# Seven block products for eight in the second MLP product of a diffusion block

## The chip, the cores and the metric

The kernel runs on one core of one Trainium2 chip. The metric is the device time in microseconds from start to end, as a median over runs. The engines are TensorE (PE, its weight loads PEld), VectorE (DVE), ScalarE (ACT), GpSimd (POOL) and SyncE (SP), on whose queue all of this kernel's transfers are started.

## The reference, cut to what matters

One block works on 1024 tokens of width 1024 in float32: a mixer (state space and attention) and then a squared-ReLU MLP of width 4096. The change touches the MLP alone:

```python
def sq_relu_mlp(h, w1, b1, w2, b2):
    return jnp.square(jax.nn.relu(h @ w1 + b1)) @ w2 + b2

h2_l = modulate(rms_norm(x, norm2_g[l]), sh2_l, sc2_l)
x = x + g2_l * sq_relu_mlp(h2_l, w_mlp1[l], b_mlp1[l], w_mlp2[l], b_mlp2[l])
```

`g2_l` is one row of 1024 gates, the last part of the modulation, which the kernel computes from `c` and `w_mod`. Call s the squared ReLU, 1024 tokens by 4096.

## The kernel before

**Exact products from rounded ones.** A float32 operand is split in two: ACT copies it to the rounded type (H), and Pool, or DVE where `low=V`, subtracts H from the raw tile to give the rest (L). Each product then takes three matmuls, H by H, H by L and L by H (`mm3`, L143 to L145, and `prod`, L1641 to L1643). `wtile` (L135, L136) loads a tile and splits it, with a row of gates multiplied in first if `scale_row` is given (L134). `wsplit` (L1665, L1666) does it for the first MLP matrix and `mq_split` (L1737, L1738) for the second. Raw tiles `wr` have three buffers, `wH` and `wL` four each. Sums come into PSUM tiles from `mmc()`, which has six buffers.

**First MLP matrix.** The 4096 columns are 32 tiles of 128, taken in 16 pairs. For 14 pairs (`NA`) the 2 x 2 block product of a pair is made with seven products instead of eight. A first pass, `first(p)`, makes two of the seven, those with the blocks B11 and B21 of h2. A second pass, `mlp1(p)`, makes the other five: T2, T1, T3, B22, T4. A turn of it is this: DVE builds from two raw weight tiles the sums `cs` (two halves, L1691 and L1692), `c4` (L1694) and `wr` (L1695); ACT and Pool split them; TensorE runs five groups of 12 matmuls; DVE forms u2, u4 and u3 (L1699 to L1702) and three `r` (L1658), ACT applies ReLU and square, and SP stores `r` to DRAM (`s_d`). `cs` and `c4` have one buffer each, so that the sums of the next pair wait until Pool has split those of the last one. In names of the listings, c is `c4`.

**Second MLP matrix.** The 32 tiles of s come back from DRAM in 15 blocks `BL`: tile 0, tile 1, 13 pairs, and the last four together. A block takes 16 PSUM groups (8 token tiles by two halves of the columns), and DVE adds each to `acc2` (L1766). In the last block it then multiplies by `g2row` (L1768) and adds the residual x2 (L1769), and SP stores the output. Between blocks 3 and 7 `mod2` makes the last part of the modulation: eight loads of 512 KB into `wr` and a DVE multiply-add after each (L1256, L1258).

**Order.** The program is written as one stream; a scheduler sets the order on each engine, and each engine runs its list in order and waits at the head of it. In the first pass TensorE's order is the written one.

Of the kernel before, what the change touches and what calls it, by code (L numbers as in the profile page):

```python
# [48 lines left out]
def block_kernel(ctx, tc, io, out, dbg=None):  # L49
# [1668 lines left out]
    def w2_src(ft):  # L1718
        return w2[ft * 128:(ft + 1) * 128, :].rearrange("p (a n) -> p a n", a=1)

    def s_src(ft):
        return s_d[ft].rearrange("p (a n) -> p a n", a=1)

    pre = [(wtile(s_src(0), (1, 1024)), wtile(w2_src(0), (1, 1024)))]
# [16 lines left out]
    def mlp2_tiles(ft):
        rs = wload(s_src(ft), (1, 1024))
        rw_ = mq.tile([128, 1024], F32, name="rw2", tag="rw2", bufs=3)
        LD.dma_start(rw_.rearrange("p (a b) -> p a b", a=1), w2_src(ft))
        return mq_split(rs, "s", 6), mq_split(rw_, "w", 6)

    BL = [[0], [1]] + [[b, b + 1] for b in range(2, 28, 2)] + [[28, 29, 30, 31]]
    NBL = len(BL)
    pre2 = [(mq_split(wload(s_src(1), (1, 1024)), "f", 2), mq_split(wload(w2_src(1), (1, 1024)), "f", 2))]
    m2_todo = list(range(30, 40))  # L1750
# [55 lines left out]
```

## Time and profile before

| | us |
|---|---|
| median of three runs | 1913.58 (1910.86 to 1914.25) |
| the profiled execution | 1909.88 |
| its span, first to last instruction | 1908.2 |
| TensorE busy | 1841.1 (96%) |
| DVE, Pool and ACT busy | 1279.1 (67%), 895.4 (47%), 691.9 (36%) |
| second pass of the first MLP matrix | about 1330 to 1543 |
| second MLP matrix, with the end | 1543 to 1908 |

The profile is one execution, read with the start of its first instruction at 0. A row of the timeline gives the start, the duration, the engine, the line, the operation with output and inputs, and in brackets how long the engine stood before it and who ended that. The granted clock (PEclk) is a share of TensorE's full 2.4 GHz; it is 0.985 over the span.

### The profile page before, as it was taken

The page shows a single profiled execution, that of the slowest core. Times are in us where ns is not written, and L with a number is a line of the kernel's source. Part 1 is how long each engine was busy: PE and PEld are TensorE (multiplying, and loading weights), DVE is VectorE, ACT ScalarE, POOL GpSimd, SP SyncE. Part 2 cuts the span into 40 slices and gives each one's busy share as a digit, 9 for nine tenths or more (in the row PEclk, how much of TensorE's full clock was granted, in tenths as well). Part 3 has the DMA queues.
Part 4 walks back from the last instruction along what each step waited for, and adds up shares of the span by engine and source line. Part 5 has one row for each costly group of instructions (what it writes and reads, how often), then busy time and mean ns, then how long its engine had stood idle before and what let it go on. Part 6 is the DMA issues. An engine that isn't in the chain of part 4 may idle for free. (4 is left out here: it accounts for less than half of the span.)

```text
span 1908.2 us, 25109 instructions
## 1 busy us (share of the span) xinstructions
PE 1841.1 (96%) x9250; PEld 1402.6 (74%) x9250; DVE 1279.1 (67%) x2194; ACT 691.9 (36%) x1016; POOL 895.4 (47%) x471
## 2 busy tenths in 40 slices
PE   7889999998999999999989999999999999999998
PEld 4668888887776556556547777887888877878887
DVE  5989998738897787777645455486454457545556
ACT  4542222244314555555442121455444541111110
POOL 2232333313425777777784453375444564443330
PEclk9989999999999999999999999999999999999999
DMA  9412222221222000000006664355554465333213
GB/s 308 97 56 71 76 77 78 76 85 46 84 71 78 18 23 23 23 23 18 22 13 207 213 209 144 116 177 182 155 155 152 126 218 178 110 107 104 89 55 144
DMA packets 179339, 200.72 MB, mean 105 GB/s; under 512 B 28112, under 2 KB 128260, under 8 KB 179216
## 3 DMA queue, kind: packets, MB, share of 16 engines
q1 hardware_dynamic: 179216, 199.11, 32.6%
q8 instruction: 73, 1.20, 0.3%
q14 instruction: 50, 0.41, 0.1%
HBM read 154.85 MB, written 44.09 MB: 104 GB/s over the span
## 5 line engine op out<-in xcount | busy, mean ns | idle before, releaser
L1202 POOL TENSOR_TENSOR accP<-accP,P 128x1024 f32<-128x1024 f32 x96 | 240.9, 2510 | 20.9 <-ACT P L1184 15.7
L1766 DVE TENSOR_TENSOR acc<-acc,mm 128x512 f32<-128x512 f32 x240 | 162.5, 686 | 127.6 <-PE mm L145 127.6
L136 POOL TENSOR_TENSOR wL<-wr,wH 128x1024 fp32r<-128x1024 f32 (+1 forms) x58 | 135.9, 2351 | 197.9 <-ACT wH L135 187.0
L1184 ACT ACTIVATE P<-sT 128x1024 f32<-128x1024 f32 x160 | 163.8, 1026 | 116.6 <-PE sT L1180 114.1
L1088 DVE TENSOR_REDUCE m<-mx 128x1 f32<-128x512 f32 x240 | 154.5, 686 | 76.1 <-PE mx L1086 69.7
L143 PE MATMUL mm<-wH,sH 128*128 128x512 f32 x480 | 187.3, 390 | 1.3 <-DVE acc L1766 1.2
L144 PE MATMUL mm<-wL,sH 128*128 128x512 f32 x480 | 186.8, 389 | 0.0
L145 PE MATMUL mm<-wH,sL 128*128 128x512 f32 x480 | 186.7, 389 | 0.0
L1197 PE MATMUL pv<-P,Vt 128*64 128x512 f32 x640 | 150.5, 600 | 0.0
L1738 POOL TENSOR_TENSOR sL<-wr,sH 128x1024 fp32r<-128x1024 f32 x30 | 72.2, 2406 | 152.0 <-ACT sH L1737 152.0
L135 ACT ACTIVATE wH<-wr 128x1024 fp32r<-128x1024 f32 (+1 forms) x62 | 61.9, 1005 | 216.2 <-PE mm L144 96.4
L1737 ACT ACTIVATE sH<-wr 128x1024 fp32r<-128x1024 f32 x30 | 31.6, 1054 | 226.5 <-issue 160.7
L1177 PE MATMUL sT<-Q,KH 128*128 128x512 f32 x320 | 105.3, 410 | 2.2 <-ACT P L1184 2.2
L143 PEld LDWEIGHTS mm<-wH,sH 128*128 128x128 f32 x480 | 90.1, 188 | 22.5 <-DVE acc L1766 2.9
L145 PEld LDWEIGHTS mm<-wH,sL 128*128 128x128 f32 x480 | 90.1, 188 | 18.9
L144 PEld LDWEIGHTS mm<-wL,sH 128*128 128x128 f32 x480 | 90.1, 188 | 18.2
L143 PE MATMUL mm<-hH,wH 128*128 128x512 f32 x248 | 101.1, 408 | 0.0
L1180 PE MATMUL sT<-Q,K 65*128 65x512 f32 x320 | 100.9, 396 | 0.0
L145 PE MATMUL mm<-hH,wL 128*128 128x512 f32 x248 | 97.7, 394 | 0.0
L144 PE MATMUL mm<-hL,wH 128*128 128x512 f32 x248 | 97.3, 392 | 0.0
L1197 PEld LDWEIGHTS pv<-P,Vt 128*64 128x64 f32 x640 | 41.7, 136 | 71.6 <-issue 62.3
L1666 POOL TENSOR_TENSOR wL<-wr,wH 128x1024 fp32r<-128x1024 f32 x32 | 76.8, 2405 | 36.6 <-ACT wH L1665 36.6
...
## 6 DMA issues: line engine op xcount, KB each, us to landing
...
```

The costliest lines, as they stand in the source:

```text
L136: (low or G).tensor_tensor(L[:, :n], raw[:, :n], H[:, :n], op=OP.subtract)
L143: T.matmul(ps, lH, rH, start=i == 0, stop=False)
L144: T.matmul(ps, lH, rL, start=False, stop=False)
L145: T.matmul(ps, lL, rH, start=False, stop=i == n - 1)
L1088: V.tensor_reduce(m3[:, 4 * j + t, c:c + 1], m, axis=AX.X, op=OP.max)
L1177: T.matmul(o, KH[kv][:, ks], Q1[:, j], start=True, stop=False)
L1180: T.matmul(o, K2[kv][:, ks], Q2[:, j], start=False, stop=True)
L1184: S.activation(P, sT, AF.Exp, scale=HD ** -0.5)
L1197: T.matmul(pv[64 * j:64 * j + 64, :], Vt[:, kt, kv * 64:kv * 64 + 64], P[:, j * 512:(j + 1) * 512], start=kt == 0, stop=kt == NK - 1)
L1202: G.tensor_tensor(accP, accP, P, op=OP.add)
L1666: (low or G).tensor_tensor(L[:, :n], raw[:, :n], H[:, :n], op=OP.subtract)
L1766: V.tensor_tensor(a_, a_ if bi else bb2[:, o], ps, op=OP.add)
```

## The change

The second MLP product gets the same treatment. Tiles 0 to 27 of s and the rows of w2 that belong to them are cut into seven blocks of 512 rows (`NB`). Each block takes seven products of 24 matmuls (four PSUM groups of six), with operands A11, A12, A22 and S1 to S4 on the side of s and B11, B21, B22 and T1 to T4 on the side of w2. The last four tiles are multiplied plainly.

- *Sums of s.* `mlp1(p)` for p below 14 reads A11 back (stored by the first pass), and builds S3 on Pool and S1, S2, S4 on DVE (L1727), which are stored to DRAM; A21 isn't stored any more. ReLU and square work in place in four tiles that the norm used before (`xs`).
- *Sums of w2.* The T blocks are DVE subtractions of 1024 columns, four a block (L1785). They are split on DVE for products 1 and 5 of a block and on Pool for the others, as are all tiles of s (L1780).
- *Sums of the products.* Each of the seven products has four tiles of its own (`X`). Block 0 is copied out of PSUM by ACT (L1824), or added to the bias by DVE (L1822); later blocks are added by DVE (L1820). Seven rounds of sums (`comb`, L1828) on DVE and Pool bring the 28 tiles to the 16 halves of the output while block 6 runs.
- *Gate.* It is multiplied into the last four tiles of w2 (L134) and, by DVE, into the sums (L1870); Pool adds x2 to these (L1871). After the last matmuls one DVE addition for each group (L1884) remains, and a store.
- *Modulation.* A piece of `mod2` now stands after every fourth product, from block 0 on.

```diff
-    s_d = dr.tile([32, 128, 1024], F32, name="s_d")
+    s_d = dr.tile([4, 128, 1024], F32, name="s_d")
+    NB = NA // 2
+    sc_d = dr.tile([NB, 7, 128, 1024], F32, name="sc_d")
+    SC = ("A11", "A12", "A22", "S1", "S2", "S3", "S4")
+    def sc_at(p, nm):
+        return sc_d[p // 2, SC.index(nm)][:, (p % 2) * 512:(p % 2) * 512 + 512]
...
+        if ft >= 2 * NA:
+            LD.dma_start(s_d[ft - 2 * NA][:, f * 512:(f + 1) * 512], r)
+        elif (ft % 2, f) != (0, 1):
+            LD.dma_start(sc_at(ft // 2, ("A11", "A12", "A22")[ft % 2 + f]), r)
...
+        if p >= NA:
+            a11 = a12 = a21 = a22 = None
+        else:
+            k = 2 * (p % 2)
+            a11, a12, a21, a22 = xs4[k][:, a], xs4[k][:, b], xs4[k + 1][:, a], xs4[k + 1][:, b]
+            LD.dma_start(a11, sc_at(p, "A11"))
+        c_out(p7, u4, 2 * p + 1, 1, a22)
+        c_out(prod(w4, 0, "B22"), u4, 2 * p, 1, a21)
+        c_out(prod(wr, 1, "T4"), u3, 2 * p + 1, 0, a12)
+        if p < NA:
+            for nm, x, y, op, E in (("S3", a11, a21, OP.subtract, G), ("S1", a21, a22, OP.add, V),
+                                    ("S2", None, a11, OP.subtract, V), ("S4", a12, None, OP.subtract, V)):
+                t = hf_tile()
+                E.tensor_tensor(t, sp_ if x is None else x, sp_ if y is None else y, op=op)
+                LD.dma_start(sc_at(p, nm), t)
+                sp_ = t
...
+    PR = [("A11", "B11"), ("A12", "B21"), ("S1", "T1"), ("S2", "T2"), ("A22", "T4"), ("S3", "T3"), ("S4", "B22")]
...
+    pre = {(0, j): (wtile(sc_src(0, PR[j][0]), (1, 1024)), wtile(w2_q(0, PR[j][1]), (2, 512))) for j in range(2)}
...
+    X = {nm: [mq.tile([128, 512], F32, name=f"X{nm}{i}") for i in range(4)] for nm, _ in PR}
...
+    def mq_split(raw, E=G):
+        H = mq.tile([128, 1024], F32R, name="fH", tag="fH", bufs=6)
+        L = mq.tile([128, 1024], F32R, name="fL", tag="fL", bufs=6)
+        S.activation(H, raw, AF.Copy)
+        E.tensor_tensor(L, raw, H, op=OP.subtract)
+        return H, L
+    def sub(x, y):
+        t = mq.tile([128, 1024], F32, name="tc", tag="tc", bufs=3)
+        V.tensor_tensor(t, x, y, op=OP.subtract)
+        return t
+    B = {}
+    def operands(b, j):
+        if j == 0:
+            for nm in ("B11", "B21", "B12", "B22"):
+                B[nm] = mq_raw(w2_q(b, nm), "rw", 7)
+        sn, tn = PR[j]
+        if tn == "T1":
+            B["T1"] = sub(B["B12"], B["B11"])
+        elif tn == "T2":
+            B["T2"] = sub(B["B22"], B["T1"])
+        elif tn == "T4":
+            B["T4"] = sub(B["T2"], B["B21"])
+        elif tn == "T3":
+            B["T3"] = sub(B["B22"], B["B12"])
+        if (b, j) in pre:
+            return pre[b, j]
+        return mq_split(mq_raw(sc_src(b, sn), "rs", 3)), mq_split(B[tn], V if j in (1, 5) else G)
+    def product(b, j, ops):
+        nm = PR[j][0]
+        (sH, sL), (tH, tL) = ops
+        for i in range(4):
+            ps = mmc()
+            prs = []
+            for h in range(2):
+                tk, o = slice(512 * h + 128 * i, 512 * h + 128 * i + 128), slice(512 * h, 512 * h + 512)
+                prs.append((sH[:, tk], sL[:, tk], tH[:, o], tL[:, o]))
+            mm3(ps, prs)
+            x = X[nm][i]
+            if b:
+                V.tensor_tensor(x, x, ps, op=OP.add)
+            elif nm in ("A11", "S1"):
+                V.tensor_tensor(x, bb2[:, 512:] if nm == "S1" else bb2[:, :512], ps, op=OP.add)
+            else:
+                S.activation(x, ps, AF.Copy)
+    def comb(out_, x, y, op=OP.add, E=V):
...
+    todo = [(b, j) for b in range(NB) for j in range(7)]
+    nxt = operands(*todo[0])
+    for n, (b, j) in enumerate(todo):
+        ops, nxt = nxt, operands(*todo[n + 1]) if n + 1 < len(todo) else None
+        product(b, j, ops)
+        if n % 4 == 3 and m2_todo:
+            mod2(m2_todo.pop(0), m2a, m2r, trc)
+            if not m2_todo:
                 LD.dma_start(g2row, bcast_rows(m2_d[3], 1024))
+        if b == NB - 1:
+            if j == 1:
+                comb("A12", "A11", "A12")
+            elif j == 3:
+                comb("S2", "A11", "S2", E=G)
+            elif j == 4:
+                comb("A11", "S2", "S1")
+            elif j == 5:
+                comb("S3", "S3", "S2", E=G)
+                comb("A22", "S3", "A22", OP.subtract)
+                comb("S1", "S3", "S1")
...
+    tiles = []
+    for ft in range(4):
+        rs = mq_split(mq_raw(one(s_d[ft]), "rs", 3))
+        r = 128 * (2 * NA + ft)
+        tiles.append((rs, wtile(one(w2[r:r + 128, :]), (1, 1024), scale_row=g2row, low=V if ft % 2 else None)))
+    comb("S4", "A11", "S4")
...
+    def base(t):
+        xr = mq.tile([128, 1024], F32, name="rw", tag="rw", bufs=7)
+        LD.dma_start(xr, x2_d[t])
+        for n in range(2):
+            o = slice(n * 512, (n + 1) * 512)
+            a_ = sums_of(t)[n]
+            V.tensor_tensor(a_, a_, g2row[:, o], op=OP.mult)
+            G.tensor_tensor(a_, a_, xr[:, o], op=OP.add)
...
+    order = [4, 5, 6, 7, 0, 1, 2, 3]
+    base(order[0])
+    for ti, t in enumerate(order):
+        if ti < 7:
+            base(order[ti + 1])
+        tk = slice(t * 128, (t + 1) * 128)
+        for n in range(2):
+            o = slice(n * 512, (n + 1) * 512)
+            ps = mmc()
+            mm3(ps, [(s_[0][:, tk], s_[1][:, tk], w_[0][:, o], w_[1][:, o]) for s_, w_ in tiles])
+            a_ = sums_of(t)[n]
+            V.tensor_tensor(a_, a_, ps, op=OP.add)
+            LD.dma_start(out_v[t][:, o], a_)
```

**DVE, one turn of the second pass.** Before:

```order
L1691 TENSOR_TENSOR cs<-wr 128x512 [waits DMAHW2_49,DVE_49,Pool_49]
L1699 TENSOR_TENSOR u_12814<-mm,t_12796 128x512 [waits PE_49]
L1692 TENSOR_TENSOR cs<-cs,wr 128x512 [waits DMAHW0_49,DVE_49]
L1695 TENSOR_TENSOR wr<-wr 128x512
L1700 TENSOR_TENSOR u_12816<-mm,u_12814 128x512 [waits DVE_49,PE_49]
L1702 TENSOR_TENSOR u_12815<-mm,u_12814 128x512 [waits PE_49]
L1658 SCALAR_TENSOR_TENSOR r<-mm,cols,u_12816 128x512 [waits DMAHW1_49,DVE_49]
L1658 SCALAR_TENSOR_TENSOR r<-mm,cols,u_12816 128x512 [waits DMAHW3_49,PE_49]
L1694 TENSOR_TENSOR c_13015<-wr,cs 128x512 [waits Pool_49]
L1658 SCALAR_TENSOR_TENSOR r<-mm,cols,u_12815 128x512 [waits DMAHW4_49,DVE_49,PE_49]
```

After (`xs` is where r goes now, and hf a sum S; the three L1727 are S1, S2 and S4):

```order
L1702 TENSOR_TENSOR cs<-wr 128x512 [waits DMAHW4_49,Pool_49]
L1703 TENSOR_TENSOR cs<-cs,wr 128x512 [waits DMAHW2_49,DVE_49]
L1706 TENSOR_TENSOR wr<-wr 128x512
L1711 TENSOR_TENSOR u_12916<-mm,u_12914 128x512 [waits PE_49]
L1713 TENSOR_TENSOR u_12915<-mm,u_12914 128x512 [waits PE_49]
L1669 SCALAR_TENSOR_TENSOR xs_10207<-mm,cols,u_12916 128x512 [waits DVE_49]
L1669 SCALAR_TENSOR_TENSOR xs_10207<-mm,cols,u_12916 128x512 [waits PE_49]
L1705 TENSOR_TENSOR c_13133<-wr,cs 128x512 [waits Pool_49]
L1727 TENSOR_TENSOR hf<-xs_10207 128x512 [waits DMAHW0_49,Activation_49]
L1669 SCALAR_TENSOR_TENSOR xs_10206<-mm,cols,u_12915 128x512 [waits DMAHW6_49,DVE_49,PE_49]
L1727 TENSOR_TENSOR hf<-hf,xs_10206 128x512 [waits DMAHW5_49,DMAHW1_49,DVE_49]
L1727 TENSOR_TENSOR hf<-xs_10206,hf 128x512 [waits DMAHW6_49,DVE_49,Activation_49]
```

The three sums stand around the last r of the turn, S1 ahead of it; u2 of the next turn, which stood behind cs, comes right after S4 and ahead of cs.

**POOL, the same turn.** Before, the splits of cs, wr and c:

```order
L1666 TENSOR_TENSOR wL_12917<-wr_12902,wH_12916 128x1024 [waits DMAHW5_49,DVE_49,Activation_49]
L1666 TENSOR_TENSOR wL_12921<-c4_12905,wH_12920 128x512 [waits DVE_49,Activation_49]
L1666 TENSOR_TENSOR wL_13021<-cs_13014,wH_13020 128x1024 [waits DVE_49,Activation_49]
L1666 TENSOR_TENSOR wL_13027<-wr_13012,wH_13026 128x1024 [waits DMAHW2_49,DVE_49,Activation_49]
L1666 TENSOR_TENSOR wL_13031<-c4_13015,wH_13030 128x512 [waits DVE_49,Activation_49]
```

After:

```order
L1727 TENSOR_TENSOR hf_12759<-xs2_10206,xs3_10207 128x512 [waits DMAHW5_49,DMAHW6_49,DMAHW3_49,Activation_49]
L1677 TENSOR_TENSOR wL_12901<-cs_12894,wH_12900 128x1024 [waits DVE_49,Activation_49]
L1677 TENSOR_TENSOR wL_12907<-wr_12892,wH_12906 128x1024 [waits DMAHW1_49,DVE_49,Activation_49]
L1677 TENSOR_TENSOR wL_12911<-c4_12895,wH_12910 128x512 [waits DVE_49,Activation_49]
L1727 TENSOR_TENSOR hf_12878<-xs0_10204,xs1_10205 128x512 [waits DMAHW5_49,DMAHW7_49,DMAHW0_49,Activation_49]
```

S3 (L1727) stands between the split of c and that of cs, and waits for ACT's square of A21.

**DVE, where the second MLP product begins.** Before, after the last r:

```order
L1658 SCALAR_TENSOR_TENSOR r<-mm,cols,u_13326 128x512 [waits DMAHW0_49,PE_49]
L1658 SCALAR_TENSOR_TENSOR r<-mm,cols,u_13325 128x512 [waits DVE_49,DMAHW2_49,PE_49,Activation_49]
L1766 TENSOR_TENSOR acc_13429<-bb_13437,mm 128x512 [waits DMAHW7_49,PE_49]
L1766 TENSOR_TENSOR acc_13429<-bb_13437,mm 128x512 [waits PE_49]
L1766 TENSOR_TENSOR acc_13430<-bb_13437,mm 128x512 [waits PE_49] x2
```

After:

```order
L1669 SCALAR_TENSOR_TENSOR r<-mm,cols,u_13453 128x512 [waits DMAHW0_49,PE_49]
L1669 SCALAR_TENSOR_TENSOR r<-mm,cols,u_13452 128x512 [waits DVE_49,DMAHW2_49,PE_49,Activation_49]
L1256 TENSOR_SCALAR m2a<-wr,sil 128x1024 [waits DMAHW3_49]
L1258 SCALAR_TENSOR_TENSOR m2a<-wr,sil,m2a 128x1024 [waits DMAHW5_49,DVE_49]
L1258 SCALAR_TENSOR_TENSOR m2a<-wr,sil,m2a 128x1024 [waits DMAHW7_49,DVE_49]
L1769 TENSOR_TENSOR bb_13596<-bb_13596 128x512 [waits DMAHW1_49]
L1822 TENSOR_TENSOR XA_13568<-bb_13596,mm 128x512 [waits PE_49]
L1822 TENSOR_TENSOR XA_13569<-bb_13596,mm 128x512 [waits PE_49]
```

Three multiplications of the modulation and a subtraction for the bias now stand ahead of the first evacuation.

**POOL, at block 6 and the last stage.** Before, the last rows of the engine:

```order
L1738 TENSOR_TENSOR wL<-rw_15639,wH 128x1024 [waits DMAHW2_49,Activation_49]
L1738 TENSOR_TENSOR sL<-wr,sH 128x1024 [waits DMAHW3_49,PE_49,Activation_49]
L1738 TENSOR_TENSOR wL<-rw_15651,wH 128x1024 [waits DMAHW4_49,Activation_49]
L1738 TENSOR_TENSOR sL<-wr,sH 128x1024 [waits DMAHW5_49,PE_49,Activation_49]
L1738 TENSOR_TENSOR wL<-rw_15663,wH 128x1024 [waits DMAHW6_49,Activation_49]
```

After (fL are splits of block 6 and the last stage, wL those of gated weights):

```order
L136 TENSOR_TENSOR wL<-wr,wH 128x1024 [waits DVE_49]
L1780 TENSOR_TENSOR fL<-rs,fH 128x1024 [waits DMAHW2_49,Activation_49]
L1780 TENSOR_TENSOR fL<-tc,fH 128x1024 [waits Activation_49,Pool_49]
L1871 TENSOR_TENSOR XA_13572<-XA_13572,rw 128x512 [waits DMAHW3_49,DVE_49]
L1780 TENSOR_TENSOR fL<-rs,fH 128x1024 [waits DMAHW5_49,Activation_49,Pool_49]
L1828 TENSOR_TENSOR XS_13580<-XA_13568,XS_13580 128x512 [waits DVE_49]
L1828 TENSOR_TENSOR XS_13581<-XA_13569,XS_13581 128x512 [waits DVE_49]
L1828 TENSOR_TENSOR XS_13582<-XA_13570,XS_13582 128x512 [waits DVE_49]
L1780 TENSOR_TENSOR fL<-rs,fH 128x1024 [waits DMAHW7_49,Activation_49,Pool_49]
L1828 TENSOR_TENSOR XS_13583<-XA_13571,XS_13583 128x512 [waits DVE_49]
L1780 TENSOR_TENSOR fL<-rw,fH 128x1024 [waits Activation_49]
L1871 TENSOR_TENSOR XA_13573<-XA_13573,rw 128x512 [waits DMAHW6_49,DVE_49]
```

Combining sums (L1828) and residual additions (L1871) stand between the splits.

## Rows read from the trace of the kernel before

**Rows 1.** Page, busy time of TensorE: us, share of the span, instructions.
```profile
PE 1841.1 (96%) x9250; PEld 1402.6 (74%) x9250; DVE 1279.1 (67%) x2194; ACT 691.9 (36%) x1016; POOL 895.4 (47%) x471
```
**Rows 2.** Stretches: us, busy PE, PEld, DVE, ACT, POOL, then clock, DMA share, GB/s.
```profile
1330.00:1540.00 210.00, 210.00 (x928) 173.95 (x927) 101.36 (x148) 98.07 (x145) 96.23 (x47) 1.00 0.49 149
...
1553.00:1558.00 5.00, 5.00 (x14) 3.91 (x13) 3.98 (x7) 3.03 (x3) 5.00 (x3) 0.54 0.95 332
```
**Rows 3.** Timeline of PE: start, duration, operation, wait before it.
```profile
1317.19 0.50 PE L1641 MATMUL mm<-T1H,wH 128*128 128x512 f32 x1 [1.50 <-DVE r L1658]
...
1417.96 0.39 PE L1641 MATMUL mm<-B22H,wH 128*128 128x512 f32 x1
...
1542.85 0.39 PE L1643 MATMUL mm<-T4L,wH 128*128 128x512 f32 x1
1543.08 0.39 PE L143 MATMUL mm<-wH 128*128 128x512 f32 x1
...
1546.93 0.39 PE L145 MATMUL mm<-wH,wL 128*128 128x512 f32 x1
1551.48 0.79 PE L143 MATMUL mm<-wH 128*128 128x512 f32 x1 [4.16 <-DVE acc L1766]
...
1557.60 0.39 PE L145 MATMUL mm<-wH,wL 128*128 128x512 f32 x1
...
1902.78 0.39 PE L145 MATMUL mm<-wH,sL 128*128 128x512 f32 x1
```
**Rows 4.** Timeline of DVE, one turn of the second pass.
```profile
1412.36 1.39 DVE L1658 SCALAR_TENSOR_TENSOR r<-mm,cols,u 128x512 f32<-128x512 f32 x2
1416.36 0.69 DVE L1694 TENSOR_TENSOR c<-wr,cs 128x512 f32<-128x512 f32 x1 [2.61 <-POOL wL L1666]
1416.97 0.74 DVE L1658 SCALAR_TENSOR_TENSOR r<-mm,cols,u 128x512 f32<-128x512 f32 x1
1421.74 1.27 DVE L1691 TENSOR_TENSOR cs<-wr 128x512 f32<-128x512 f32 x1 [4.02 <-DMA wr<-in_w_mlp_dram]
1422.93 0.68 DVE L1699 TENSOR_TENSOR u<-mm,t 128x512 f32<-128x512 f32 x1
...
1425.93 0.74 DVE L1658 SCALAR_TENSOR_TENSOR r<-mm,cols,u 128x512 f32<-128x512 f32 x1
```
**Rows 5.** Timeline of POOL, the same turn.
```profile
1415.02 1.30 POOL L1666 TENSOR_TENSOR wL<-c,wH 128x512 fp32r<-128x512 f32 x1 [6.13 <-ACT wH L1665]
1417.16 2.41 POOL L1666 TENSOR_TENSOR wL<-cs,wH 128x1024 fp32r<-128x1024 f32 x1 [0.83 <-ACT wH L1665]
1420.07 2.39 POOL L1666 TENSOR_TENSOR wL<-wr,wH 128x1024 fp32r<-128x1024 f32 x1 [0.51 <-ACT wH L1665]
```
**Rows 6.** Instructions of L1691 and L1214: count, ns min/median/max, starts, forms.
```profile
L1691 DVE TENSOR_TENSOR cs<-wr x16: 676/1222/1483, 1302.5 to 1505.7; 128x512 f32<-128x512 f32 x16
...
L1214 DVE TENSOR_TENSOR accD<-accD,accP x8: 1217/2876/2876, 630.8 to 972.2; 128x1024 f32<-128x1024 f32 x8
```
**Rows 7.** Timeline of all engines at 1253 us.
```profile
1252.36 1.75 POOL L1575 TENSOR_TENSOR hf<-hf 128x512 f32<-128x512 f32 x1
...
1252.99 1.67 DVE L1574 TENSOR_TENSOR hf<-hf,B11L 128x512 f32<-128x512 f32 x1
...
1254.08 1.74 POOL L1570 TENSOR_TENSOR B22L<-hf,B22H 128x512 fp32r<-128x512 f32 x1
```
**Rows 8.** Timeline of DVE: first evacuation of the second product, and the end.
```profile
1550.73 5.68 DVE L1766 TENSOR_TENSOR acc<-bb,mm 128x512 f32<-128x512 f32 x9 [6.65 <-DMA bb<-in_b_mlp_dram]
...
1903.93 0.69 DVE L1768 TENSOR_TENSOR acc<-acc,g2row 128x512 f32<-128x512 f32 x1
1904.65 0.69 DVE L1769 TENSOR_TENSOR acc<-acc,rw 128x512 f32<-128x512 f32 x1
```
**Rows 9.** Timeline of ACT, the turn of group 4.
```profile
1415.50 0.63 ACT L1650 ACTIVATE r<-r 128x512 f32<-128x512 f32 x1
...
1418.95 1.05 ACT L1665 ACTIVATE wH<-wr 128x1024 fp32r<-128x1024 f32 x1
```

More of the change, by code (lines that the diff above doesn't have):

```diff
@@ L1715, in block_kernel, with one, w2_q, sc_src @@
         mlp1(p)
[L1718 to L1724, printed above, removed]
+    PR = [("A11", "B11"), ("A12", "B21"), ("S1", "T1"), ("S2", "T2"), ("A22", "T4"), ("S3", "T3"), ("S4", "B22")]
+    def one(src):
+        return src.rearrange("p (a n) -> p a n", a=1)
+    def w2_q(b, nm):
+        e, h = int(nm[1]) - 1, int(nm[2]) - 1
+        return w2[512 * b:512 * b + 512, 512 * h:512 * h + 512].rearrange("(j e p) n -> e p j n", e=2, p=128)[e]
+    def sc_src(b, nm):
+        return one(sc_d[b, SC.index(nm)])
+    pre = {(0, j): (wtile(sc_src(0, PR[j][0]), (1, 1024)), wtile(w2_q(0, PR[j][1]), (2, 512))) for j in range(2)}
     ml_.__exit__(None, None, None)
@@ L1741, in mlp2_tiles @@
[L1741 to L1750, printed above, removed]
@@ L1751, in block_kernel @@
     m2a = mq.tile([128, 1024], F32, name="m2a")
     m2r = mq.tile([128, 512], F32, name="m2r")
-    for bi, fts in enumerate(BL):
-        last_ = bi == NBL - 1
-        tiles = (pre, pre2)[bi] if bi < 2 else [mlp2_tiles(ft) for ft in fts]
-        for t in range(8):
-            if last_:
-                xr = mq.tile([128, 1024], F32, name="rw2", tag="rw2", bufs=3)
-                LD.dma_start(xr, x2_d[t])
-            tk = slice(t * 128, (t + 1) * 128)
-            for n in range(2):
-                o = slice(n * 512, (n + 1) * 512)
-                ps = mmc()
-                mm3(ps, [(s_[0][:, tk], s_[1][:, tk], w_[0][:, o], w_[1][:, o]) for s_, w_ in tiles])
-                a_ = acc2[t][:, o]
-                V.tensor_tensor(a_, a_ if bi else bb2[:, o], ps, op=OP.add)
-                if last_:
-                    V.tensor_tensor(a_, a_, g2row[:, o], op=OP.mult)
-                    V.tensor_tensor(a_, a_, xr[:, o], op=OP.add)
-                    if t == 7:
-                        LD.dma_start(out_v[t][:, o], a_)
-            if last_ and t < 7:
-                LD.dma_start(out_v[t], acc2[t])
-        if 3 <= bi < 8:
-            for _ in range(2):
-                mod2(m2_todo.pop(0), m2a, m2r, trc)
-            if bi == 7:
-                LD.dma_start(g2row, bcast_rows(m2_d[3], 1024))
@@ new lines, in block_kernel, with mq_raw @@
+    LD.dma_start(bb2, bcast_rows(io["b_mlp2"], 1024))
+    V.tensor_tensor(bb2[:, 512:], bb2[:, 512:], bb2[:, :512], op=OP.subtract)
+    def mq_raw(src, tag, bufs):
+        r = mq.tile([128, 1024], F32, name=tag, tag=tag, bufs=bufs)
+        LD.dma_start(r.rearrange("p (a n) -> p a n", n=src.shape[-1]), src)
+        return r
+    def mq_split(raw, E=G):
[4 more added lines that the diff above has]
+        return H, L
@@ new lines, in block_kernel, with sums_of @@
+    tiles = []
[4 more added lines that the diff above has]
+    comb("S4", "A11", "S4")
+    def sums_of(t):
+        return [X["A12"][t], X["S4"][t]] if t < 4 else [X["A22"][t - 4], X["S1"][t - 4]]
+    def base(t):
[6 more added lines that the diff above has]
+            G.tensor_tensor(a_, a_, xr[:, o], op=OP.add)
```

19 lines of the change are left out of this document (5 added, 14 removed).

## The prediction

> **What bounds the kernel now.** I read the page first, then the work by stretches, and then one turn of the last pass over the first MLP matrix on each engine. TensorE is busy 96% of the span, and in the stretch from 1330 to 1540 us it never stops [rows 1, 2]; so a matmul removed is time removed, as long as nobody else becomes late. A 512-column matmul starts 0.2265 us after the one before it (17 steps between 1543.08 and 1546.93, [rows 3]); the duration printed beside it is longer, since matmuls overlap. I take 0.2267, which also gives the turn: 60 matmuls, 13.60 us.
>
> The other engines look half idle, but not in the turn. Counting from the first r at 1412.36, DVE does two r, waits 2.6 us for Pool, does c (L1694) at 1416.36, the last r, waits 4.0 us for a load, does cs at 1421.74, and comes to the next r at 1425.93, after 13.57 us [rows 4]. That is TensorE's turn to 0.03 us. Of slack there is only this: wL of c ends at 1416.32 [rows 5] and TensorE wants it at 1417.96 [rows 3], 1.6 us.
>
> What matters most is a side effect in these rows. A DVE operation whose inputs are both in SBUF doesn't run while Pool runs, nor the other way about. L1691 takes 0.68 us at best and 1.22 at the median; the instance at 1421.74 ends 0.55 us after the Pool operation of 1420.07 does (1423.01 against 1422.46). L1214 takes 1.22 alone and 2.88 at worst [rows 6]. In the stretch at 1253 both engines have such work queued, and they take turns strictly: DVE 1.67 a piece, Pool 1.74 a piece, though alone they take 0.68 and 1.30 [rows 4 to 7]. DVE operations that read PSUM are untouched: r at 1416.97 takes 0.74 under Pool's operation of 1417.16. So DVE's SBUF work and all of Pool's work share one resource ("the port" below). Once waiting, a piece costs 0.55 (DVE 512 wide, the row at 1421.74), and for the others I take 0.1 off the unhindered rows: 1.08 (DVE 1024), 1.17 (Pool 512) and 2.3 (Pool 1024; 2.35 where Pool runs on alone).
>
> The Trainium skill says this too (SBUF — State Buffer, section Who interferes with whom): a DVE instruction with two SBUF inputs and a GpSimd instruction that reads SBUF exclude each other for the whole instruction, and the order of issue decides who blocks. The trace agrees (1.22 against 0.68); the page doesn't say who follows, the rows at 1253 show turns. It speaks against this change, which puts sums on both engines; were it wrong, the two stages below would lose nothing and the second rival's sum would stand.
>
> **The change part by part.**
>
> *Matmuls.* The second product takes 1536 now (last of the first matrix 1542.85, first of the second 1543.08, last 1902.78, [rows 3]): 348.2 us at 0.2267 in a stretch of 359.9. It will take 7 x 7 x 24 + 192 = 1368. 168 x 0.2267 = **-38.1 us**, certain if TensorE stays the bound. At the end of the kernel a group needs one DVE operation after its last matmul, not three: two of 0.69 with a step of 0.03 each, **-1.4** [rows 8].
>
> *The turn.* Each of the first 14 pairs gains three DVE sums and one Pool sum (S3), all on SBUF, a load and two more stores. The transfers are cheap there: DMA is at 49% in that stretch [rows 2]. Pool's four operations fill 1.17 x 2 + 2.3 x 2 = 6.9 us, so by plain addition all fits. The order decides. With 0 at the first r and the rows' durations:
> - wL of c runs 2.66 to 3.96 as now. S3 stands right behind it. Its last input, the square of A21, is ready at 3.77 (ACT 1415.50 + 0.63, [rows 9]), so S3 starts at about 3.91, before c, which is told of wL's end at 4.00. c waits to 5.2, ends at 5.75.
> - wL of cs, long ready, takes the port 5.75 to 8.05. S1, next on DVE, waits for it and ends at 8.60. The last r stands behind S1: 8.5 to 9.25 (in the trace it ends at 5.35). S2 to 9.85.
> - ACT's relu and square of that r end at 10.58, S4 follows to 11.3, u2 to 11.9. ACT's split of wr stands behind that square and ends at 11.6; wL of wr holds the port to 13.95, so cs waits again: 13.95 + 0.5, then cs, wr, u4, u3 at 0.6 each, and the next r is at 16.85.
>
> A turn of 16.85 in place of 13.60, 3.25 more. Of 14 pairs some 12 turns are full ones: 12 x 3.25 less the slack of 1.6 = **+37.4 us**. No engine is full in this; it is a chain of waits around the loop. Bounds: 0 if everything fits, +14 with c ahead of S3 (below), and 46 with 14 turns.
>
> *Start of the second product.* Now TensorE stops for 4.16 us at 1551.48 since the first evacuation waits for the bias until 1550.73 [rows 3, 8], and then runs at half clock (granted 0.54 from 1553 to 1558, [rows 2]); the 14 steps from 1551.48 to 1557.60 take 6.12 us and not 3.17 [rows 3]. Together 7.1; of the 11.7 that the stretch lasts beyond its matmuls 4.6 are left for small waits later on, and I give 2 of these to the start. In the new order three operations of the second modulation that wait for loads stand ahead of the first evacuations on DVE, and four w2 quarters and the S loads come after them on SP. From the last store to the third product's operands: bias, three modulation tiles, four quarters, two S tiles, 10 x 0.52 MB at 332 GB/s [rows 2] = 15.8 us, then a subtraction, ACT's split and Pool's, 1.1 + 1.05 + 2.3, [rows 5, 9], and ahead of it all 5 us in which the last stores come through the queue: 25.3 us after the last matmul of the first matrix. The two ready products cover 10.9. A stall of 14.4 and 2.9 of half clock against 9.1: **+8**. Bounds 0 and +14.
>
> *Blocks 1 to 5.* Per block Pool has 12 pieces and DVE 6 of 1024: 12 x 2.35 + 6 x 1.08 = 34.7 of 38.1 us. It fits narrowly, and the modulation's pieces come on top in the first two blocks: **+1.5**, bounds 0 and 4.
>
> *Block 6 and the last stage.* Here the combining sums, four gated weight tiles and the sums' gate and residual all come at once. From the first split of block 6 to the last split of the fourth tile Pool has 18 pieces of 1024 and 11 of 512, 54.3 us; DVE's SBUF work among them is 9 of 1024 and 28 of 512, 25.1. The port needs 79.4 us. It can begin two products (10.9 us, less 1 of evacuation) before block 6, since six buffers allow no more. The last stage's first group can't end until the fourth tile is split: 79.4 - 9.9 = 69.5, and 0.9 for its last matmuls, after block 6 begins, where TensorE alone needs 38.1 + 2.7. **+29.6**, and 1.4 of half clock if these stalls are long: **+31**. Bounds: 0, if the order lets the splits by, and 36.
>
> Sum: -38.1 - 1.4 + 37.4 + 8 + 1.5 + 31 = +38.4 on the profiled execution's 1909.9, 1948.3. The median shown lies 3.7 above that execution: **1952**; I say 1951.
>
> **The rivals.**
> 1. *c gets the port ahead of S3.* It hangs on 0.1 us. Then S1 starts at 5.85, the last r at 6.4, wL of wr ends at 12.2 and the turn is about 14.9: 12 x 1.3 - 1.6 = 14. For it: one load or ACT operation late is enough. Against: Pool's next operation starts without a message from another engine (1254.08, 0.03 before the modelled end of the one ahead, [rows 7]). 1951 - 23 = 1928.
> 2. *Faster: the sums fit the gaps.* DVE idles 2.6 + 4.0 us a turn [rows 4] and its three sums take 2.0; Pool idles 6.1 between two splits [rows 5]. If loads, not the port, set DVE's order in time, or the last stage's splits run ahead, neither stage loses: 1909.9 - 39.5 + 9.5 + 3.7 = 1884. It decides where the exclusion ends a wait that a load would have ended anyway, as it does at 1421.74 by half a microsecond. Against: c has no load ahead of it and 1.6 us of slack.
> 3. *The end is milder.* The sums for pairs of products may find holes while TensorE waits; 10 in place of 31: 1930.
> 4. *The clock falls in the turns.* A TensorE gap of 4.16 us was followed by half speed, one of 1.50 at 1317.19 was not [rows 3]. If the 3.25 us collect in one gap, 14 matmuls a turn take 2.9 us more; where the turn's own waits hide a third, 12 x 2 = 24: 1975.
>
> **How the numbers follow.** Forecast 50%, 1938 to 1964. Rival 1, 14%; rival 3, 13%; both of these together 3%, 1907; rival 2, 12%; rival 4, 8%. Range 1907 to 1972: it leaves out rival 2 and most of 4. 0.2%, which is about what a measurement here can tell, is 4 us: faster is rival 2 and the 3% (0.15); within it is what the mixtures of rivals 1 and 2 leave (0.04); slower 0.81.
>
> **What would show it.** In the changed trace: matmuls of the second product 0.227 apart and 1368 of them; u (L1710) every 16.8 us in the turns (13.6 refutes the turn, 14.9 is rival 1); c (L1705) of about 1.7 us and S1 of some 2.9, waiting under Pool; TensorE stalled about 14 us soon after the second product begins; and some 30 us of TensorE waits for fL and wL between block 6 and the last stage, with DVE sums of 1.7 us beside Pool sums of 1.7. Wrong it would be above all if DVE sums under Pool's run at 0.6.

## The result, and the profile after

The changed kernel takes 1960.76 us (median of four runs, 1959.96 to 1963.54) against 1913.91 for the kernel before: a ratio of 1.025, with a 95% interval of 1.023 to 1.027. It is slower by 47 us although it does 168 matmuls less. The forecast was 1951, in a range of 1907 to 1972.

Two lines of the page of the changed kernel, busy time by engine, answer to [rows 1]:

```profile
span 1956.9 us, 24984 instructions
...
PE 1823.1 (93%) x9082; PEld 1365.9 (70%) x9082; DVE 1435.5 (73%) x2224; ACT 744.2 (38%) x1078; POOL 1052.2 (54%) x536
```

TensorE has 18 us less to do, DVE and Pool are each busy for more than 150 us more, and the span is 48.7 us longer. Busy time isn't work alone: an operation that has started and waits under the other engine's counts as busy (a sum of 0.68 us can show as 2.88). The stretches show where TensorE waits. The rows give us, then busy PE, PEld, DVE, ACT, POOL, the granted clock, DMA's share and GB/s; they are the second pass over the first MLP matrix, then of the second product block 0, block 1, blocks 2 to 4, block 5, block 6, and the last stage:

```profile
1330.00:1540.00 210.00, 182.69 (x757) 138.99 (x756) 168.68 (x160) 75.26 (x111) 97.47 (x51) 1.00 0.54 180
1581.60:1635.10 53.50, 40.64 (x169) 32.72 (x168) 31.72 (x23) 26.36 (x36) 36.82 (x14) 0.87 0.72 252
1635.10:1681.10 46.00, 40.21 (x169) 31.00 (x169) 43.55 (x39) 14.54 (x15) 36.48 (x13) 1.00 0.59 214
1681.10:1798.70 117.60, 115.83 (x505) 94.13 (x504) 87.92 (x103) 42.22 (x42) 95.84 (x36) 1.00 0.43 148
1798.70:1839.20 40.50, 40.50 (x174) 31.59 (x174) 26.15 (x34) 15.03 (x16) 29.46 (x12) 1.00 0.46 155
1839.20:1900.40 61.20, 43.53 (x170) 31.49 (x168) 52.47 (x47) 17.96 (x18) 50.90 (x23) 0.97 0.26 92
1900.40:1956.90 56.50, 48.05 (x192) 38.44 (x192) 39.81 (x44) 0.00 (x0) 30.28 (x17) 0.89 0.23 84
```

The first row is the same stretch as in [rows 2]: TensorE was busy for all 210 us there and is now for 182.7. A block is 168 matmuls, 38.1 us of work; block 0 takes 53.5, block 6 takes 61.2.

One turn of the second pass on DVE, from one u (L1710) to the next (1456.68), and Pool's four operations in it. These rows answer to [rows 4] and [rows 5]:

```profile
1439.74 0.68 DVE L1710 TENSOR_TENSOR u<-mm,t 128x512 f32<-128x512 f32 x1
1440.34 2.73 DVE L1702 TENSOR_TENSOR cs<-wr 128x512 f32<-128x512 f32 x1
...
1445.51 1.40 DVE L1669 SCALAR_TENSOR_TENSOR xs<-mm,cols,u 128x512 f32<-128x512 f32 x2
1449.48 1.76 DVE L1705 TENSOR_TENSOR c<-wr,cs 128x512 f32<-128x512 f32 x1 [2.57 <-POOL wL L1677]
1451.17 2.88 DVE L1727 TENSOR_TENSOR hf<-xs 128x512 f32<-128x512 f32 x1
1453.97 0.74 DVE L1669 SCALAR_TENSOR_TENSOR xs<-mm,cols,u 128x512 f32<-128x512 f32 x1
1454.63 0.68 DVE L1727 TENSOR_TENSOR hf<-hf,xs 128x512 f32<-128x512 f32 x1
1456.07 0.69 DVE L1727 TENSOR_TENSOR hf<-xs,hf 128x512 f32<-128x512 f32 x1 [0.76 <-ACT xs L1658]
```

```profile
1440.12 2.40 POOL L1677 TENSOR_TENSOR wL<-wr,wH 128x1024 fp32r<-128x1024 f32 x1 [3.57 <-ACT wH L1676]
1448.18 1.27 POOL L1677 TENSOR_TENSOR wL<-c,wH 128x512 fp32r<-128x512 f32 x1 [5.66 <-ACT wH L1676]
1449.41 1.29 POOL L1727 TENSOR_TENSOR hf<-xs,xs 128x512 f32<-128x512 f32 x1
1450.66 2.84 POOL L1677 TENSOR_TENSOR wL<-cs,wH 128x1024 fp32r<-128x1024 f32 x1
```

S3 starts at 1449.41 and c at 1449.48, 0.07 us later; c ends 0.54 us after S3 does (1451.24 against 1450.70). Then S1 waits under the split of cs, the last r stands behind S1, S4 waits for ACT's square of that r, and cs waits under the split of wr. The turn is 16.94 us. No row here is a large piece of work; what is long are four rows, cs (2.73), c (1.76), S1 (2.88) and Pool's split of cs (2.84). Operations of the same shapes take 0.68 to 0.69 on DVE and 2.40 on Pool here where nobody is in the way.

In the second product these are the waits of TensorE (timeline, rows with a wait only, some left out):

```profile
1602.83 1.22 PE L143 MATMUL mm<-fH 128*128 128x512 f32 x2 [10.23 <-ACT fH L1779]
1606.68 0.79 PE L144 MATMUL mm<-fL,fH 128*128 128x512 f32 x1 [2.63 <-POOL fL L1780]
...
1888.01 0.47 PE L143 MATMUL mm<-fH 128*128 128x512 f32 x1 [2.45 <-DVE XA L1820]
1893.85 0.50 PE L143 MATMUL mm<-fH 128*128 128x512 f32 x1 [1.14 <-DVE XS L1820]
1900.39 0.77 PE L143 MATMUL mm<-wH,fH 128*128 128x512 f32 x1 [4.89 <-DVE XS L1820]
1904.81 0.50 PE L145 MATMUL mm<-wH,fL 128*128 128x512 f32 x1 [0.81 <-POOL fL L1780]
1909.24 0.79 PE L145 MATMUL mm<-wH,fL 128*128 128x512 f32 x1 [3.47 <-POOL fL L1780]
```

The page names DVE's additions of products as the releaser in block 6. They have a PSUM input and take 0.67 themselves; what holds them is what stands ahead of them on DVE, sums and weight tiles under the lock. A piece of both engines from there, DVE and then Pool:

```profile
1880.98 2.28 DVE L1828 TENSOR_TENSOR XA<-XS,XS 128x512 f32<-128x512 f32 x1
1883.18 0.67 DVE L1820 TENSOR_TENSOR XA<-XA,mm 128x512 f32<-128x512 f32 x1
1884.42 2.85 DVE L1828 TENSOR_TENSOR XA<-XS,XS 128x512 f32<-128x512 f32 x1 [0.56 <-POOL XS L1828]
1887.19 0.68 DVE L1820 TENSOR_TENSOR XA<-XA,mm 128x512 f32<-128x512 f32 x1
```

```profile
1879.87 2.84 POOL L1780 TENSOR_TENSOR fL<-rs,fH 128x1024 fp32r<-128x1024 f32 x1
1882.67 1.72 POOL L1828 TENSOR_TENSOR XS<-XA,XS 128x512 f32<-128x512 f32 x1
1884.35 2.37 POOL L1780 TENSOR_TENSOR fL<-rw,fH 128x1024 fp32r<-128x1024 f32 x1
```

The sum at 1884.42 begins 0.07 us after Pool's split of 1884.35 and ends 0.55 after it (1887.27 against 1886.72).

### The profile page after: what moved, and what is told of

Read it like the earlier page. It is cut to its first block, busy times and chain, and to the rows that moved or that the text cites. A ratio compares the mean times of both kernels' runs of the same rounds, so it can differ in the third digit from the quotient of the medians.

```text
span 1956.9 us, 24984 instructions
## 1 busy us (share of the span) xinstructions
PE 1823.1 (93%) x9082; PEld 1365.9 (70%) x9082; DVE 1435.5 (73%) x2224; ACT 744.2 (38%) x1078; POOL 1052.2 (54%) x536
## 5 line engine op out<-in xcount | busy, mean ns | idle before, releaser
L136 POOL TENSOR_TENSOR wL<-wr,wH 128x1024 fp32r<-128x1024 f32 (+1 forms) x62 | 147.7, 2389 | 200.9 <-ACT wH L135 189.9
L143 PE MATMUL mm<-fH 128*128 128x512 f32 x376 | 150.4, 401 | 30.2 <-DVE XA L1820 11.2
L1780 POOL TENSOR_TENSOR fL<-rs,fH 128x1024 fp32r<-128x1024 f32 x51 | 141.5, 2776 | 56.8 <-issue 29.4
L144 PE MATMUL mm<-fL,fH 128*128 128x512 f32 x376 | 148.2, 394 | 3.0 <-POOL fL L1780 3.0
L145 PE MATMUL mm<-fH,fL 128*128 128x512 f32 x376 | 147.9, 393 | 0.0
L1779 ACT ACTIVATE fH<-rs 128x1024 fp32r<-128x1024 f32 x51 | 54.0, 1059 | 165.7 <-issue 113.5
L143 PEld LDWEIGHTS mm<-fH 128*128 128x128 f32 x376 | 71.4, 190 | 56.8 <-ACT fH L1779 13.5
L1197 PEld LDWEIGHTS pv<-P,Vt 128*64 128x64 f32 x640 | 41.7, 136 | 71.6 <-issue 62.3
L212 PE MATMUL mm<-wL,hH 128*128 128x512 f32 (+1 forms) x216 | 83.2, 385 | 8.9 <-POOL wL L136 8.8
L1177 PEld LDWEIGHTS sT<-Q,KH 128*128 128x128 f32 x320 | 55.1, 188 | 50.4 <-issue 26.0
L210 PE MATMUL mm<-wH,hH 128*128 128x512 f32 (+1 forms) x216 | 82.4, 384 | 4.7 <-DVE qn L983 2.9
```

Of the source, the lines that this page charges most:

```text
L136: (low or G).tensor_tensor(L[:, :n], raw[:, :n], H[:, :n], op=OP.subtract)
L143: T.matmul(ps, lH, rH, start=i == 0, stop=False)
L144: T.matmul(ps, lH, rL, start=False, stop=False)
L145: T.matmul(ps, lL, rH, start=False, stop=i == n - 1)
L212: T.matmul(ps, lH, wL[:, o], start=False, stop=k == 7)
L1177: T.matmul(o, KH[kv][:, ks], Q1[:, j], start=True, stop=False)
```

## The experiments

The theory to be tested: in the turns and around block 6 the time goes into the exclusion between DVE operations with two SBUF inputs and Pool's operations. The rivals: the amount of work on DVE or its chain through ACT; the transfers; the modulation. The runs were on several chips, on which the kernel before took 1907.5 to 1913.1, so the lengths of stages within a profile are compared rather than totals. Each run is a single execution, except the last with everything together. What an edit leaves alone repeats well: in the first three runs and in that of the sums of products block 0 takes 53.5 to 54.2 us and block 1 46.0 to 46.6, and in the first three the stretch from the start of block 6 to the second token tile of the last stage takes 75.0 or 75.1 (75.3 in the changed kernel). That stretch is 168 and 24 matmuls, 43.5 us for TensorE alone; the expectations call its end the last stage's second product.

**Sums left out, transfers kept.**

```diff
-                t = hf_tile()
-                E.tensor_tensor(t, sp_ if x is None else x, sp_ if y is None else y, op=op)
+                t = {"S3": a21, "S1": a22, "S2": a11, "S4": a12}[nm]
```

> The four sums of s (S1 to S4) are left out of the second pass: the raw tiles are stored in their place, so the number and size of the transfers stay and the second product works on wrong operands. Port theory: the turn goes from 16.95 us back to TensorE's 13.6, the first MLP matrix ends some 38 to 40 us earlier, and the kernel takes about 1922 us; the second product keeps its 371 us. Rival, transfers (an added load and two added stores a pair) or ReLU and square in other tiles make the turn long: the turn stays above 15.5 and the time above 1945.

Measured 1925.9 us. The turn is 13.57 us, as in the kernel before, for nine turns on end. Two early ones take 19.7 and 20.3: there DVE's cs waits 10.66 and 5.90 us for a weight tile to land, and what made these two loads late stays open. From the first u2 to the second product it is 220.6 us, against 257.1 in the changed kernel and 214.6 before, so 36.5 of the 42.6 us go with the sums. The added load and stores of each pair and the work in other tiles cost nothing in a steady turn, and the rival of the transfers falls for those; they may have a part in the two early turns. The second product took 370.9, unchanged.

**S3 on DVE.** The one edit is `("S3", a11, a21, OP.subtract, V)` for `G`.

> S3 is moved from Pool to DVE; the same four sums, all with both inputs in SBUF. Port theory: c is no longer behind S3 under the lock, but DVE's sums still wait under Pool's two long splits, so the turn falls only in part, to about 16 us, and the time to about 1947. Rival, it is the amount of work on DVE: DVE has one operation more, the turn becomes 17.5 or longer and the time 1968 or more. Rival, Pool's S3 alone is to blame: turn 13.6, time 1922.

Measured 1949.3, with a turn of 15.77 us. c takes 0.69 and S3 too, but S1 takes 2.90 under the split of cs, and the second half of cs 2.72 under that of wr:

```profile
1433.61 2.90 DVE L1727 TENSOR_TENSOR hf<-xs 128x512 f32<-128x512 f32 x1
1439.74 2.72 DVE L1703 TENSOR_TENSOR cs<-cs,wr 128x512 f32<-128x512 f32 x1
```

With one operation more on DVE the turn got shorter, so DVE's load doesn't set it; and S3 on Pool was a third of the loss (1.2 of 3.4 us), not all.

**A21 in PSUM.** ACT's square of A21 goes to a PSUM tile, and S1 and S3 read it there:

```diff
+        q21 = None if p >= NA else trc()
+        c_out(prod(w4, 0, "B22"), u4, 2 * p, 1, a21, q21)
...
+            for nm, x, y, op, E in (("S3", a11, q21, OP.subtract, V), ("S1", q21, a22, OP.add, V),
```

> All four sums on DVE as in the run with S3 on DVE, but ACT writes the square of A21 into a PSUM tile, so that S1 and S3 have one input in PSUM and one in SBUF. Same number of operations on DVE and ACT. Port theory: S1 and S3 take 0.7 us also under Pool's operations, the turn is 13.6 to 14, the time about 1920 to 1925. Rival, the amount of work or the chain through ACT's squares sets the turn: no difference from the run with S3 on DVE.

Measured 1924.9, with a turn of 13.80. The number of operations on DVE and ACT is that of the run before it; the edit changes only where one tile stands, and the turn falls by 2 us. The scheduler's order on DVE is another too (the last r stands ahead of S1 now, and S4 and u2 ahead of cs), so that not all of the 2 us need come from the port; the rows show the port by themselves. DVE's rows of it (L1728 are S3, S1, S2, S4 in this order), and Pool's split that runs beside them:

```profile
1433.25 0.69 DVE L1705 TENSOR_TENSOR c<-wr,cs 128x512 f32<-128x512 f32 x1 [2.60 <-POOL wL L1677]
1433.86 0.68 DVE L1728 TENSOR_TENSOR hf<-xs,tr 128x512 f32<-128x512 f32 x1
1434.46 0.74 DVE L1669 SCALAR_TENSOR_TENSOR xs<-mm,cols,u 128x512 f32<-128x512 f32 x1
1435.12 0.68 DVE L1728 TENSOR_TENSOR hf<-tr,xs 128x512 f32<-128x512 f32 x1
1435.83 1.18 DVE L1728 TENSOR_TENSOR hf<-hf,xs 128x512 f32<-128x512 f32 x1
```

```profile
1434.05 2.42 POOL L1677 TENSOR_TENSOR wL<-cs,wH 128x1024 fp32r<-128x1024 f32 x1 [0.83 <-ACT wH L1676]
```

S1 (1435.12, one input `tr` in PSUM) takes 0.68 in the middle of Pool's split; S2 behind it, both inputs in SBUF, waits for the split's end at 1436.47 and ends 0.54 later. This pair of neighbouring rows is the cleanest evidence for the theory, since no order or load comes into it.

**Gate not folded.** Gate and residual come after the last matmuls, on DVE, as in the kernel before:

```diff
-        tiles.append((rs, wtile(one(w2[r:r + 128, :]), (1, 1024), scale_row=g2row, low=V if ft % 2 else None)))
+        tiles.append((rs, wtile(one(w2[r:r + 128, :]), (1, 1024), low=V if ft % 2 else None)))
...
+            V.tensor_tensor(a_, a_, g2row[:, o], op=OP.mult)
+            V.tensor_tensor(a_, a_, xr[:, o], op=OP.add)
```

> The gate is no longer multiplied into the last four weight tiles and into the sums, and x2 is not added ahead of the last stage: as in the kernel before, DVE multiplies and adds after each group of the last stage. Port theory: four pieces of 1024 and 16 pairs of 512 leave the port, some 15 us of them ahead of the last stage; the stall between block 6 and the last stage falls from 32 us to 15 to 20, two DVE operations come back at the end (+1.4), time about 1948. Rival, late loads or the modulation hold the last stage: stall unchanged, time 1962.

Measured 1950.7. From the start of block 6 to the second token tile of the last stage, where TensorE alone needs 43.5 us, the changed kernel takes 75.3 and this one 56.8: the stall falls from 31.8 to 13.3. But more than the gate's and the residual's operations left the stretch. The last four weight tiles need no gate row here, and the scheduler put their splits into block 1, which got 3.3 us longer; two of the four rows:

```profile
1669.32 1.21 DVE L136 TENSOR_TENSOR wL<-wr,wH 128x1024 fp32r<-128x1024 f32 x1
1678.34 2.83 DVE L136 TENSOR_TENSOR wL<-wr,wH 128x1024 fp32r<-128x1024 f32 x1
```

In the changed kernel these splits run from 1841 to 1873, in block 6. So the run doesn't tell what those operations are worth alone.

**Five of seven splits of w2 on DVE**, `V if j in (0, 1, 2, 4, 5)` for `(1, 5)`.

> Five of the seven w2 operands of a block are split on DVE, not two (products 0, 1, 2, 4, 5). A split holds the port for 1.1 us on DVE and 2.35 on Pool, so a block asks for 3.8 us less port time, about 31 of 38.1; DVE gets more work. Port theory: blocks 2 to 4 fall from 39.2 to 38.1 us, block 1 from 46.0 to about 44, and block 6 with the first group of the last stage gets some 5 us shorter; the second product takes about 360 us instead of 371. Rival, DVE's amount of work or late loads set the blocks: no gain, or up to 10 us more.

The second product takes 359.3 instead of 371.0. Blocks 2 to 4 are at 38.1, without any wait of TensorE (busy 114.60 of 114.60 us), block 1 at 41.7, and the stretch from block 6 to the last stage's second token tile is 4.3 us shorter. DVE does more and none of these stages gets longer. The run takes work off Pool's queue as well as off the lock; in blocks 2 to 4 Pool's own pieces (12 of 2.35 us in 38.1) don't fill its time, so that the shorter hold, 1.1 us instead of 2.35, is the likelier cause there.

```profile
1637.80:1679.50 41.70, 39.97 (x171) 31.02 (x169) 41.58 (x42) 14.56 (x15) 26.59 (x9) 1.00 0.62 214
1679.50:1794.10 114.60, 114.60 (x507) 94.91 (x506) 97.46 (x113) 42.57 (x43) 66.31 (x27) 1.00 0.47 152
```

**Modulation left out**: `m2_todo = []`, and the gate row read from the bias.

> The last part of the modulation is left out (ten pieces on DVE with their loads, and its matmuls); the gate row is read from the bias instead. Theory that the modulation's pieces hold the first evacuations and the loads: block 0 falls from 53.6 to about 46 us and block 1 from 46.0 to about 41. Rival, the loads of the new operands and Pool's splits of them set the start and block 1 anyway: both stay within 2 us, and the second product at 369 to 372.

Block 0 took 56.1, block 1 42.5, and the stretch from block 6 to the last stage's second token tile 63.6 instead of 75.3. That was inconclusive for the start: with the gate row there from the beginning, the scheduler put the gated weight tiles where the modulation had stood, so that the loads and waits ahead of the first evacuations were others and not fewer. And it raised a question, whether the gain of 12 us at the end came from the missing pieces or from the early gate.

**Modulation left out, gate late**, made from two sums of block 5:

```diff
+        if n == 39:
+            for h in range(2):
+                V.tensor_tensor(g2row[:, 512 * h:512 * h + 512], X["A22"][h], bb2[:, :512], op=OP.add)
```

> The last part of the modulation is left out again, but now the gate row is made late, from sums of block 5 (so the output is another), so that the gated weights stay where they are in the changed kernel. The three loads at the start stay too: they are those of weight tiles. Theory A, the modulation's pieces on DVE cost block 1 and not the start, and the gain at the end in the run without the modulation came from the early gate: block 0 within 1.5 us of 53.6, block 1 41 to 43 instead of 46, last stage's second product as far after the start of block 6 as in the changed kernel (75 us). Theory B, the waiting modulation pieces ahead of the first evacuations make the start long: block 0 at 49 or less.

Block 0 took 55.7, block 1 39.2, and the stretch at the end 74.6. Block 0 got 2 us longer and block 1 shorter than theory A had them, but its signs hold in each part: the modulation's pieces cost block 1 nearly 7 us, nothing at the start, nothing at the end; the 11 to 12 us were the early gate, which lets four gated tiles be split long before block 6.

**Fewer loads ahead of the start.** Modulation and last weights use the buffers of the w2 quarters:

```diff
-            w = wp.tile([128, 1024], F32, name="wr", tag="wr", bufs=3)
+            w = wp.tile([128, 1024], F32, name="wr", tag="wr", bufs=3) if raw is None else raw()
...
+            mod2(m2_todo.pop(0), m2a, m2r, trc, lambda: mq.tile([128, 1024], F32, name="rw", tag="rw", bufs=7))
```

> Modulation tiles and the last weight tiles are loaded into the buffers of the w2 quarters and no longer into those of the first MLP matrix, so that three loads of 512 KB no longer stand ahead of the operands at the start; nothing is left out. Theory that the queue of loads sets the start: block 0 falls from 53.6 to about 50 (three loads at 1.6 us), later blocks may get longer since the quarters' buffers are shared. Rival, the first evacuations on DVE set it: block 0 stays within 1 us.

Block 0 took 50.3 and TensorE's first wait 5.80 us instead of 10.23. The rows of TensorE in this run:

```profile
1602.89 1.22 PE L143 MATMUL mm<-fH 128*128 128x512 f32 x2 [5.80 <-ACT fH L1779]
1606.77 0.79 PE L144 MATMUL mm<-fL,fH 128*128 128x512 f32 x1 [2.66 <-POOL fL L1780]
```

So the queue of loads sets the start: the first wait falls by 4.4 us, 1.5 for each of the three loads, close to the 1.6 that the rate in [rows 2] gives, and block 0 by 3.3. Block 1 fell to 41.9 as well, block 3 rose to 43.7, and the total was 1960.6, on a chip where the kernel before took 1913.1.

**Sums of products on DVE alone** (`E=G` dropped in two `comb` calls).

> The eight sums of products that Pool makes in block 6 are made by DVE. A piece holds the port for 0.55 us there and 1.17 on Pool, 5 us in all. Port theory: block 6 and the last stage get 5 us shorter, the second product 366 instead of 371. Rival, DVE is the bound there (it has eight operations more): 371 or longer.

The second product took 364.6, 6.4 us less; from block 6 to the last stage's second token tile 66.7 instead of 75.3. Again more work on DVE and a shorter stall, though here too Pool's queue lost the work that the lock lost.

**All together**: A21 in PSUM, sums of products on DVE, five splits on DVE, gate not folded.

> All that took load off the port, together: S1 and S3 from PSUM, sums of products on DVE, five splits of w2 on DVE, gate and residual after the last matmuls as in the kernel before. Port theory: the turn is 13.8 us, the second product 340 to 346 us, the end 1.4 us longer, so about 27 to 30 us less than the run with A21 in PSUM alone, 1895 to 1899 on the chip of that run, where the kernel before took 1907.5: ratio 0.993 to 0.996. If the parts only move the wait to DVE: 1910 or more.

Measured 1894.2 us (four runs, 1890.6 to 1896.6) beside 1910.0 for the kernel before on that chip: a ratio of 0.991, interval 0.988 to 0.994. The turn is 13.80 and the second product takes 342.3 us, both as expected. The version is 0.9% faster than the kernel before. Page, and the stretches of block 0, block 1, blocks 2 to 4, block 6:

```profile
PE 1811.5 (96%) x9082; PEld 1372.9 (72%) x9082; DVE 1418.5 (75%) x2278; ACT 744.9 (39%) x1078; POOL 932.9 (49%) x478
```

```profile
1546.40:1599.60 53.20, 41.48 (x170) 33.26 (x169) 37.36 (x26) 26.37 (x37) 30.06 (x11) 0.87 0.78 271
1599.60:1644.40 44.80, 40.74 (x170) 30.71 (x169) 44.24 (x41) 18.45 (x19) 34.45 (x11) 1.00 0.56 197
1644.40:1758.70 114.30, 114.30 (x506) 94.63 (x505) 97.85 (x115) 42.26 (x43) 66.48 (x28) 1.00 0.49 158
...
1799.10:1843.40 44.30, 40.47 (x170) 32.41 (x168) 43.57 (x44) 14.07 (x14) 29.02 (x11) 0.96 0.35 116
```

Pool is busy 119 us less than in the changed kernel, DVE 17 less, and TensorE is back at 96%. What is left of the cost are block 0 (15 us over its work), block 1 (7) and the stretch from block 6 to the last stage's second token tile (51.4, 8 over its work).

## Why the prediction was right, point by point

| step | forecast | measured in the profile |
|---|---|---|
| matmuls | -38.1 | -38.1 |
| one operation, not three, at the end | -1.4 | -0.9 |
| turns of the second pass | +37.4 | +42.6 |
| start of the second product | +8 | +7.4 |
| blocks 1 to 5 | +1.5 | +10.0 |
| block 6 and last stage | +31 | +31.8 |
| all before the second pass | 0 | -4.1 |
| sum | +38.4 | +48.7 |

*Turns: right in mechanism and order, and nearly in size.* The forecast turn was 16.85, the rows give 16.94 to 16.96, with each wait where it was put: c of 1.76 (forecast about 1.7), S1 of 2.88 (2.9), cs under the split of wr. The rival that c comes first hung on 0.1 us; S3 was ahead by 0.07. From the first u2 to the first matmul of the second product it is now 257.1 us, before 214.6. Of the 42.6 more, 12 turns of 3.38 (16.95 against 13.57) make 40.6; the slack of 1.6 that the sum took off helped nobody, and the first and last turns, which it left out, cost 2.0.

*Start: right in size, and for half of its reason.* TensorE waits 12.9 us in two gaps and runs at half clock after them (granted 0.50 from 1602.83 to 1610, 0.87 over block 0); block 0 is 15.5 us longer than its matmuls. In the kernel before the first 168 matmuls took 46.2, 8.1 more than their work; the forecast had put 9.1 there. The queue of loads sets this, as the sum over ten loads had it, and the third product began 21.3 us after the last matmul of the first matrix, forecast 25.3. The modulation's operations ahead of the first evacuations, which the step named too, cost nothing there: without them, and with loads of other tiles in their place, block 0 took 55.7.

*Blocks 1 to 5: the mis-sized step.* It set port time against a block's length, 34.7 of 38.1, and took 1.5 us for the rest, with 4 as its bound. Blocks 2 to 4 lost 1.1 each, so narrow room isn't free room: pieces come in an order, and a wait of 3.4 us for one is passed on. Block 1 lost 7.9, since five pieces of the modulation stand in it close together: four multiply-adds of 2.2 to 3 us each under the lock and an addition of 3.00. They were known from the order and were put down as "on top" without a sum. Without them block 1 takes 39.2. The rows of block 1:

```profile
1637.90 5.99 DVE L1258 SCALAR_TENSOR_TENSOR m2a<-wr,sil,m2a 128x1024 f32<-128x1024 f32 x2 [0.71 <-DMA wr<-in_w_mod_dram]
1647.73 2.83 DVE L1258 SCALAR_TENSOR_TENSOR m2a<-wr,sil,m2a 128x1024 f32<-128x1024 f32 x1
1651.68 2.21 DVE L1258 SCALAR_TENSOR_TENSOR m2a<-wr,sil,m2a 128x1024 f32<-128x1024 f32 x1
1657.75 3.00 DVE L1264 TENSOR_TENSOR m2a<-m2a,wr 1x1024 f32<-1x1024 f32 x1
```

Block 5 is 2.3 us over its work without any wait (TensorE busy 40.50 of 40.50 us): four matmuls of the modulation (L1266) stand in it. From the 13.6 us of these blocks go 3.6 that the kernel before lost later on as well, 1.9 of them on the same four matmuls.

*Block 6 and the last stage: right in mechanism; that the size agrees so closely is partly luck.* 31.8 against 31. From the first split of block 6 (1828.32) to the end of the last tile's split (1909.19) it is 80.9 us, and the forecast had 79.4 of lock for it. Of its pieces, Pool's 18 wide and 11 narrow ones and DVE's 9 wide ones are there, but only 17 of DVE's 28 narrow ones; the others came after. At the forecast's prices that is 73.4 us of lock, and most of the rest are gaps, 6.4 us in all, in which neither engine held it. The lock was taken for more than nine tenths of the stretch, and so it sets its length. Three runs that took lock time away shortened it, not each by the forecast: 5 us less by forecast gave 8.6 (sums on DVE) and 5 gave 4.3 (splits). The 18.5 for 15 (gate not folded) is no test of the account, since four splits left the stretch as well. What the step didn't see is that the place of the four gated tiles is worth 11 to 12 us by itself: they wait for the gate row, which comes at the end of block 5, and so their work falls into the fullest stretch. Of the two runs without the modulation, the one with the early gate row took 63.6 for the stretch and the one with the late row 74.6.

*End.* The last addition ends the chain as forecast, but the store after it lands later: 3.3 us from its issue at 1953.56 to the end of the span, against 2.8 before (1905.38). The gain was 0.9.

*The total, partly luck.* For the steps from the second pass on the forecast was 14.4 us too low in all. The part ahead of the second pass, which the change leaves alone, happened to be 4.1 us shorter in this profile than before, and that hid as much of the miss.

*The faster rival* (1884, the sums fit the gaps) was wrong for this order of instructions and right about what is possible: with two sums taken off the lock the turn is 13.80, 0.2 us from TensorE's own. The clock in the turns didn't fall (granted 1.00 from 1330 to 1540): the 3.4 us are spread over several gaps, of which 1.51 (at 1445.14) and 0.85 (at 1449.51) are the longest in the turn shown. What the Trainium skill's rule on the shared port (SBUF — State Buffer, section Who interferes with whom) says of DVE instructions with at most one SBUF input, that outside the engine's 2-port modes they don't contend, is what the run with A21 in PSUM shows as well (S1 0.68 beside S2 1.18).
